# A two-by-two block scheme with seven products for the feed-forward of a hybrid trunk

## The chip, the cores and the metric

One Trainium2 chip, of which the kernel uses 1 core. The metric is the device time of one execution in microseconds, as the median of 3 runs.

## The reference

Two layers over 256 context tokens and 1024 latent tokens (1280 in all) of width 1024. Each layer is a mixer (layer 0: gated position mixing and grouped-query attention; layer 1: neighbourhood attention) and then a SwiGLU feed-forward with hidden width 2816. Both have a normed and modulated input and a normed and gated output:

```python
def swiglu(h, w_in, w_out):
    g, u = jnp.split(h @ w_in, 2, axis=-1)
    return (jax.nn.silu(g) * u) @ w_out
...
        fp = swiglu(sublayer_in(xp, norm_ffn_pre[l], fsh_p, fsc_p), ffn_w_in[l], ffn_w_out[l])
        fs = swiglu(sublayer_in(xs, norm_ffn_pre[l], fsh_s, fsc_s), ffn_w_in[l], ffn_w_out[l])
        xp = sublayer_out(xp, fp, norm_ffn_post[l], fgt_p)
        xs = sublayer_out(xs, fs, norm_ffn_post[l], fgt_s)
```

Everything is float32.

## The kernel before

**Precision.** A float32 product is made of three matrix products. `split` (L147 to L154) writes an operand as a high part (a cast, on ACT or DVE) and a low part (a subtraction of two SBUF tiles, on DVE or POOL), and `mm3_steps` (L168 to L170) adds high x high, high x low and low x high in PSUM.

**Feed-forward before.** The normed input lies transposed in the tiles `hh` and `hl` for the whole feed-forward (8 k tiles x 1280 tokens, both parts). A hidden tile `m` of 22 is 128 hidden columns: `wload` brings a gate unit, an up unit and an output unit (128 x 1024 each) from `wall` and splits them on ACT and POOL. `product` computes gate and up for a chunk of tokens (512, 512 or 256): 2 x 8 k tiles x 3 matmuls. `gating` takes silu, the product and a split. `output` multiplies each 128-token tile with the output unit, in two halves of 512 columns, 3 matmuls each, and DVE adds each half from PSUM to the running sum `y` (L1075), which stays in SBUF. So a hidden tile costs TensorE 48 weight tiles over 1280 tokens and 60 matmuls of 512 columns. The last three hidden tiles go chunk by chunk, so that the closing norms of the first chunks (L1090, L1097, L1105, and for layer 0 the transposes of `prenorm_cols`) go among the other chunks' products; in layer 0 the first products of the next mixer (`first_products`) go there too. `extra` makes six vectors of the modulation among the products of layer 0 and one in layer 1 (`mod_steps`, L224, on DVE).

**Ahead of it** `out_proj` goes tile by tile over 128 tokens; `cols` turns each normed tile into `hh` and `hl`, and for the last two tiles that step comes after the feed-forward's first item.

**Rooms.** The pools that matter: `s5` (17 tiles of 5 KB a partition), `wt` (8 of 4 KB), `raw` (3 of 4 KB), `t2` (5 of 2 KB), and eight PSUM banks: tag A (2 tiles of two banks), B (3 of one) and C (1). All transfers are issued from SP's queue. Outside the stretches whose order is written out by hand, a scheduler places the instructions of each engine by priority (program order) as their inputs come ready.

Of the kernel before, what the change touches and what calls it, by code (L numbers as in the profile page):

```python
# [18 lines left out]
P = 128  # L19
# [8 lines left out]
# So many of the feed-forward's hidden tiles come chunk by chunk.  # L28
LAST = 3
DEFER = 2  # L30
AFTER = 0
# [5 lines left out]
# Weight units of 128 x 1024 in the order of use.  # L37
# [12 lines left out]
def trunk_kernel(ctx: ExitStack, tc: tile.TileContext, A: dict, O: dict):  # L50
# [50 lines left out]
    # Scale and shift of the normed input: layer, sub-layer, condition, (A, B), k tile.  # L101
# [9 lines left out]
    # Sums over the partitions, to row 0 or row 1.  # L111
# [28 lines left out]
    def pipeline(items, *stages):  # L140
        """Each stage, (lag, function), on each item, lag steps behind the first."""
# [6 lines left out]
    def split(hi, lo, src, eng=None, hi_eng=None):  # L148
        """hi + lo = src, 12 bits each."""
# [14 lines left out]
    def mm3_steps(out, terms, per=1000):  # L164
        """Float32 products of operands that come as two 12-bit parts each."""
        n = len(terms)
        for i, (sh, sl, mh, ml) in enumerate(terms):
            PE.matmul(out, sh, mh, start=i == 0, stop=False)  # L168
            PE.matmul(out, sh, ml, start=False, stop=False)  # L169
            PE.matmul(out, sl, mh, start=False, stop=i == n - 1)  # L170
# [7 lines left out]
    def rstd_of(ss, n, scale, eps=EPS):  # L178
        """(ss * scale + eps) ** -0.5"""
        v, r = sm(n), sm(n)  # L180
        DVE.tensor_scalar(v, ss, scale, eps, op0=ALU.mult, op1=ALU.add)
        POOL.tensor_tensor(r, v, mhalf[:, 0:n], op=ALU.pow)  # L182
        return r

# [73 lines left out]

    def mods_of(*parts):
        return filler(itertools.chain(*(mod_steps(l, part) for l, part in parts)))  # L260

# [12 lines left out]
    def prenorm_cols(t, xh, l, w, wide, lo=None):  # L274
        """xh scaled, shifted and transposed, to hh and hl."""
# [15 lines left out]
    def gate_load(l, w, r):  # L291
        g = s5([P, D])
# [6 lines left out]
    def x_load(src):  # L299
        xt = raw([P, D])  # L300
        SP.dma_start(xt, src)
        return xt

    def postnorm(y, xt, gate, dst):
        """x + gate * normed y, to dst; returns it."""
# [3 lines left out]
        DVE.tensor_tensor(nx, nx, xt, op=ALU.add)  # L309
# [7 lines left out]
    def halves(base):  # L317
# [12 lines left out]
    def put_o(o, dst, base):  # L330
        """Sum of the two halves of o, to partitions base.. of dst."""
# [4 lines left out]
    class Job:  # L336
        """Heads' attention for two tiles of queries, step by step: keys on the free axis for the
        softmax, then turned in groups to meet the values."""

        def pair(self):  # L340
            """Room for two parts of a group."""
# [3 lines left out]
        def turn(self, i):  # L345
            """groups[i]: which output, and [(key tile, [(query tile, column)])]."""
# [43 lines left out]
    def run_jobs(jobs, slots, depth, extra, engines):  # L390
        """jobs(n): the n-th job or None at the end. Each goes on for depth periods of so many slots."""
# [21 lines left out]
    # ================= layer 0, mixer =================  # L413
# [34 lines left out]
    # Norm gains of keys and of queries, these times 1/8.  # L448
# [4 lines left out]
    def head_squares(n, src, nh, tmp):  # L453
        """Per-head norm, and rotary of latents, of src, [P, nh * 64] in PSUM: four parts."""
# [33 lines left out]
    def in_proj_rows(acc, t, units, nk, n):  # L488
        """acc[tok, n] = h W for one tile of tokens; units of nk k tiles each."""
# [7 lines left out]
    # Keys and values of both heads.  # L497
# [90 lines left out]
    def cache_steps():  # L588
        """The cache's keys and values."""
# [1094 lines left out]
```

## Time and profile before

| | |
|---|---|
| median of 3 runs | 3514.62 us (3513.19 to 3517.15) |
| profiled execution, span | 3511.9 us |
| TensorE (PE) busy | 3329.4 us, 95% |
| VectorE (DVE) busy | 2175.8 us, 62% |
| ScalarE (ACT) busy | 1319.9 us, 38% |
| GpSimd (POOL) busy | 1222.6 us, 35% |
| transfers | 260.19 MB, mean 74 GB/s |

The profiled execution's own time is known by its span, from the first to the last instruction; the runs' times hold the little that lies around it as well, so the median stands 2.7 us above the span. Feed-forward 0 runs from about 752 us to about 1724 us of the span, feed-forward 1 from about 2577 us to the end. A matmul's shown duration is a latency: matmuls overlap, and their cost is the distance from start to start.

### The profile page before, as it was taken

The numbers are of one execution on the slowest core, as the hardware profiler recorded it, in microseconds if no ns is written. First come the engines' busy times: TensorE is split into PE (matmuls) and PEld (weight loads), VectorE is DVE, ScalarE is ACT, GpSimd is POOL, SyncE is SP. The second block draws the span as 40 slices with busy tenths as digits, with TensorE's granted clock in tenths as the row PEclk, the third lists the DMA queues.
The fourth block names the chain that finished last, engine by engine and source line by source line (L and its number), as shares of the span: only waits on it lengthen the run. The fifth ranks groups of instructions, "written<-read, shape, count | busy, mean of one in ns | idle before, by whom it ended". The sixth has DMA issues, their size and how long they took to land. (4 is left out here: it accounts for less than half of the span.)

```text
span 3511.9 us, 46282 instructions
## 1 busy us (share of the span) xinstructions
PE 3329.4 (95%) x17930; PEld 2790.1 (79%) x17930; DVE 2175.8 (62%) x3749; ACT 1319.9 (38%) x2561; POOL 1222.6 (35%) x822
## 2 busy tenths in 40 slices
PE   6889899999999999999899999998999999999998
PEld 3667787887877878887788888887877888888886
DVE  7879998546666664445767777777574444443447
ACT  3467863441111111113666666666541111111123
POOL 3556666451111111124644444444221111111134
PEclk7889999999999999999999999999999999999999
DMA  5210033432222221113311111113331111111124
GB/s 207 65 37 13 19 95 123 155 123 85 90 86 81 85 86 39 44 51 132 124 40 45 44 45 44 45 44 102 108 131 57 36 37 36 39 45 38 37 85 167
DMA packets 106621, 260.19 MB, mean 74 GB/s; under 512 B 10640, under 2 KB 46352, under 8 KB 106400
## 3 DMA queue, kind: packets, MB, share of 16 engines
q1 hardware_dynamic: 106400, 257.23, 22.7%
q8 instruction: 141, 2.31, 0.3%
q14 instruction: 80, 0.66, 0.1%
HBM read 221.37 MB, written 35.82 MB: 73 GB/s over the span
## 5 line engine op out<-in xcount | busy, mean ns | idle before, releaser
L1075 DVE TENSOR_TENSOR s<-s,B 128x512 f32<-128x512 f32 x840 | 559.5, 684 | 568.2 <-PE B L170 567.3
L154 POOL TENSOR_TENSOR w<-raw,w 128x1024 fp32r<-128x1024 f32 x163 | 403.7, 2479 | 1412.0 <-ACT w L153 1406.9
L168 PE MATMUL A<-hh,w 128*128 128x512 f32 (+1 forms) x2112 | 755.5, 358 | 3.9 <-ACT w L153 2.4
L170 PE MATMUL A<-hh,w 128*128 128x512 f32 (+1 forms) x2112 | 750.4, 355 | 3.0 <-POOL w L154 3.0
L169 PE MATMUL A<-hl,w 128*128 128x512 f32 (+1 forms) x2112 | 747.9, 354 | 0.0
L168 PEld LDWEIGHTS A<-hh,w 128*128 128x128 f32 x2112 | 397.8, 188 | 69.8 <-issue 5.9
L170 PEld LDWEIGHTS A<-hh,w 128*128 128x128 f32 x2112 | 397.4, 188 | 66.4 <-POOL w L154 4.4
L169 PEld LDWEIGHTS A<-hl,w 128*128 128x128 f32 x2112 | 397.5, 188 | 62.8
L153 ACT CAST w<-raw 128x1024 fp32r<-128x1024 f32 x166 | 174.1, 1049 | 718.5 <-PE B L169 398.8
L168 PE MATMUL B<-w,s 128*128 128x512 f32 x880 | 351.2, 399 | 15.1 <-DVE s L1075 14.7
L170 PE MATMUL B<-w,s 128*128 128x512 f32 x880 | 348.1, 396 | 12.2 <-DVE s L154 10.2
L1056 ACT ACTIVATE t<-A,c 128x512 f32<-128x512 f32 (+1 forms) x132 | 81.1, 615 | 704.2 <-PE A L170 704.2
L169 PE MATMUL B<-w,s 128*128 128x512 f32 x880 | 344.1, 391 | 0.0
L352 PE MATMUL B<-c,s 128*128 128x128 f32 x1568 | 238.7, 278 | 40.4 <-DVE w L368 23.4
L368 DVE TENSOR_TENSOR t<-B,t 128x512 fp32r<-128x512 f32 (+1 forms) x248 | 162.3, 654 | 143.9 <-ACT t L362 140.3
L352 PEld LDWEIGHTS B<-c,s 128*128 128x128 f32 x1568 | 181.2, 141 | 83.2 <-DVE w L368 35.7
L168 PE MATMUL C<-hh,w 128*128 128x512 f32 (+1 forms) x576 | 211.6, 367 | 3.4 <-ACT s L1321 2.2
L1057 DVE TENSOR_TENSOR t<-t,A 128x512 f32<-128x512 f32 (+1 forms) x132 | 78.9, 597 | 217.4 <-ACT t L1056 217.4
L168 PEld LDWEIGHTS B<-w,s 128*128 128x128 f32 x880 | 165.4, 188 | 59.1 <-DVE s L1075 27.2
L170 PEld LDWEIGHTS B<-w,s 128*128 128x128 f32 x880 | 165.5, 188 | 55.3 <-DVE s L154 15.6
L170 PE MATMUL C<-hh,w 128*128 128x512 f32 (+1 forms) x576 | 205.3, 356 | 0.0
L169 PE MATMUL C<-hl,w 128*128 128x512 f32 (+1 forms) x576 | 205.0, 356 | 0.0
(285 smaller groups left out, 6473.1 us busy)
## 6 DMA issues: line engine op xcount, KB each, us to landing
raw<-wall SPq DMA_DIRECT2D x171, 512.0 KB, 3.5
raw<-mod_w SPq DMA_DIRECT2D x72, 512.0 KB, 4.0
x_d<-s SPq DMA_DIRECT2D x30, 512.0 KB
w<-wall SPq DMA_DIRECT2D x22, 512.0 KB, 3.7
raw<-x SPq DMA_DIRECT2D x20, 512.0 KB, 4.2
s<-x_d SPq DMA_DIRECT2D x20, 512.0 KB, 6.5
s<-wall SPq DMA_DIRECT2D x17, 512.0 KB, 6.0
w<-mod_w SPq DMA_DIRECT2D x16, 512.0 KB, 10.0
```

Source lines behind the costliest of these rows:

```text
L153: ACT.copy(hi, src)
L154: (eng or DVE).tensor_tensor(lo, src, f32(hi), op=ALU.subtract)
L168: PE.matmul(out, sh, mh, start=i == 0, stop=False)
L169: PE.matmul(out, sh, ml, start=False, stop=False)
L170: PE.matmul(out, sl, mh, start=False, stop=i == n - 1)
L352: PE.transpose(tr[:, at : at + P], self.p[a][:, col : col + P], ident)
L368: DVE.tensor_tensor(tl[:, 0:n], tr[:, 0:n], f32(th[:, 0:n]), op=ALU.subtract)
L1056: ACT.activation(s, acc[:, 0, 0:n], AF.Silu, bias=zerob)
L1057: DVE.tensor_tensor(s, s, acc[:, 1, 0:n], op=ALU.mult)
L1075: DVE.tensor_tensor(yt, yt, part, op=ALU.add)
```

## The change

For both matrix products of the feed-forward the operands are seen as two-by-two blocks, and the four block sums, of eight block products, are made from seven. The blocks of the tokens are even and odd tiles of 128 tokens, those of the inner axis are halves (k tiles 0 to 3 and 4 to 7; even and odd hidden tiles for the second product), those of the columns are gate and up (for the second product the two halves of 512).

- `prenorm_pair`: an odd tile's first four k tiles are stored as the difference to the even tile. `out_proj` goes in `OUT_ORDER`.
- Stage one (`step`, 22 hidden tiles): seven products of 4 k tiles x 3 matmuls, over token sets of 384 and of 256. Three operands more of the tokens (`sums`) lie in 12 of the 17 `s5` tiles. `weights` makes seven split operands of a hidden tile, `collect` the sums, the gating and the store of the inner activations to DRAM (`gu_d`), unsplit.
- Stage two: for two pairs of hidden tiles at a time `down_load` brings the activations and output units back, `down_split` makes the operands in `hh` and `hl`, which are free by then, and `group` goes over five pairs of token tiles in three groups of products. The eleventh pair of hidden tiles comes last, pair of token tiles by pair, with the closing norms behind each (`tail_...`). The next mixer's first products come in the program behind all that.
- `behind` holds the first instructions of the feed-forward behind the last ones of `out_proj` on their engines; `mod_half_steps` makes the modulation in halves of 512 columns.

```diff
+SETS = (slice(2, 5), slice(0, 2))
...
+    def prenorm_pair(t, xh, l, w, lo):
...
+        if t % 2 == 0:
+            split(hh[:, :, rows(t)], hl[:, :, rows(t)], xh, lo, DVE)
+        else:
+            split(hh[:, 4:8, rows(t)], hl[:, 4:8, rows(t)], xh[:, 4:8], lo, DVE)
+            for x in (hh, hl):
+                DVE.tensor_tensor(xh[:, 0:4], xh[:, 0:4], f32(x[:, 0:4, rows(t - 1)]), op=ALU.subtract)
+            split(hh[:, 0:4, rows(t)], hl[:, 0:4, rows(t)], xh[:, 0:4], lo, DVE)
...
+    PRODUCTS = ((1, 0), (5, 2), (2, 0), (3, 2), (6, 1), (7, 1), (4, 1))
+    def three(out, a, b, start):
...
+            for j, (x, z) in enumerate(((ah, bh), (ah, bl), (al, bh))):
+                PE.matmul(out, x, z, start=start and i + j == 0, stop=i == n - 1 and j == 2, skip_group_check=True)
...
+        more = [[[s5([P, 2, 640], F32R) for _ in range(2)] for _ in range(2)] for _ in range(3)]
+        def sums(s):
...
+            for k in range(4):
...
+                DVE.tensor_tensor(x, b22[0], t1[0], op=ALU.subtract)
+                DVE.tensor_tensor(d, b22[1], t1[1], op=ALU.subtract)
+                DVE.tensor_tensor(x, x, d, op=ALU.add)
+                split(*parts[0], x, DVE)
+                POOL.tensor_tensor(z, b21[0], x, op=ALU.subtract)
+                POOL.tensor_tensor(z, z, b21[1], op=ALU.add)
+                split(*parts[2], z, POOL)
+                for v in b11:
+                    DVE.tensor_tensor(x, x, v, op=ALU.subtract)
+                split(*parts[1], x, DVE)
...
+        def weights(m, i):
+            g, u = st["gu", m, 0], st["gu", m, 1]
+            if i == 5:
...
+            elif i == 3:
+                DVE.tensor_tensor(g[:, 1], g[:, 1], g[:, 0], op=ALU.subtract)
...
+            st["w", m, i] = o = wt([P, 2, 512], F32R)
+            split(o[:, 0], o[:, 1], src, POOL)
...
+            elif i == 6:
+                DVE.tensor_tensor(uv[:, 0], x, z[:, 0], op=ALU.add)
+                DVE.tensor_tensor(uv[:, 0], y, uv[:, 0], op=ALU.add)
+                ACT.activation(uv[:, 0], uv[:, 0], AF.Silu, bias=zerob)
+            elif i == 7:
+                DVE.tensor_tensor(uv[:, 1], x, z[:, 0], op=ALU.add)
+                POOL.tensor_tensor(z[:, 1], uv[:, 1], z[:, 1], op=ALU.add)
+                POOL.tensor_tensor(z[:, 1], uv[:, 0], z[:, 1], op=ALU.mult)
+            elif i == 4:
+                DVE.tensor_tensor(z[:, 0], x, z[:, 0], op=ALU.add)
+                DVE.tensor_tensor(z[:, 0], z[:, 0], z[:, 2], op=ALU.mult)
+                SP.dma_start(gu_d[l][m][:, :, c], z[:, 0:2])
...
+        def step(m, i, where):
+            for s in range(2):
+                product(m, i, where, s)
+                collect(m, i, s)
+            if m < MT - 1:
+                weights(m + 1, i)
+            extra(2 if i == 1 else 1)
+        for fn in before:
+            fn()
+        with behind(("SP", "DVE", "PE")):
+            weights_load(0)
+            for i, _ in PRODUCTS:
+                weights(0, i)
+            sums(0)
+            weights_load(1)
+            for i, where in PRODUCTS:
+                if i == 6:
+                    sums(1)
+                step(0, i, where)
...
+        PAIRS = (1, 2, 3, 4, 0)
+        GROUPS = (((1, 0), (2, 1)), ((5, 2), (3, 3)), ((6, 4), (7, 5), (4, 6)))
...
+        def down_ready(j, i):
...
+            if i == 5:
+                st["gs", j] = s5([P, 640])
+                DVE.tensor_tensor(st["gs", j], ge[:, 1], go[:, 1], op=ALU.add)
+                DVE.tensor_tensor(ge[:, 1], ge[:, 0], ge[:, 1], op=ALU.subtract)
+                DVE.tensor_tensor(ge[:, 0], st["gs", j], ge[:, 0], op=ALU.subtract)
+                POOL.tensor_tensor(we[:, 0], we[:, 1], we[:, 0], op=ALU.subtract)
+            elif i == 3:
+                DVE.tensor_tensor(go[:, 0], go[:, 0], ge[:, 0], op=ALU.subtract)
+            elif i == 6:
+                POOL.tensor_tensor(we[:, 1], wo[:, 1], we[:, 1], op=ALU.subtract)
+                POOL.tensor_tensor(wo[:, 1], wo[:, 1], we[:, 0], op=ALU.subtract)
+            elif i == 4:
+                POOL.tensor_tensor(wo[:, 0], wo[:, 0], wo[:, 1], op=ALU.subtract)
...
+        def down_split(js, g, at):
...
+                    split(ah[:, 0], ah[:, 1], a, POOL if g == 2 else DVE)
+                    split(bh[:, 0], bh[:, 1], b, POOL)
...
+        def group(g, ops):
...
+                three(banks[q], *cuts, k == 0)
+                down_collect(q, i, banks[q])
...
+        for c, js in enumerate(chunks):
+            for g in range(3):
+                now = ready
+                if g < 2:
+                    at = 8 - at
+                    ready = down_split(js, g + 1, at)
+                else:
...
+                group(g, now)
...
+        def tail_tokens(q):
...
+            for n, i in enumerate((1, 2, 5, 3, 6, 7, 4)):
+                a, _ = tail_ready(i, place[q])
+                o = ops[n // 4][:, n % 4]
+                split(o[:, 0], o[:, 1], a, DVE)
...
+        def tail_products(q):
...
+                three(banks[where], [(ops[i][:, 0], ops[i][:, 1])], [(tail_w[i][:, 0], tail_w[i][:, 1])], i in (1, 5, 6))
+                down_collect(q, i, banks[where])
+            z = first_sum[q]
+            POOL.tensor_tensor(e[:, 1], e[:, 1], z, op=ALU.add)
+            POOL.tensor_tensor(o[:, 1], o[:, 1], z, op=ALU.add)
+            DVE.tensor_tensor(o[:, 0], o[:, 0], z, op=ALU.add)
...
+        for n, q in enumerate(PAIRS):
+            if n + 1 < len(PAIRS):
+                tail_tokens(PAIRS[n + 1])
...
+            tail_products(q)
+            for t in (2 * q, 2 * q + 1):
+                tail_norm(t)
+                if l == 0:
+                    tail_cols(t)
```

`down_collect` adds a product's bank to its sum by one DVE instruction of 128x512, as L1075 does before. `weights` for product 5 has three sums of 128x512 on DVE. `tail_norm` has for each tile a square sum (ACT), one product with the gate (DVE or POOL, by turns) and one fused multiply and add (DVE).

## Rows read from the trace of the kernel before

**Rows 1.** The page: span, and busy time, share and instructions by engine.

```profile
span 3511.9 us, 46282 instructions
...
PE 3329.4 (95%) x17930; PEld 2790.1 (79%) x17930; DVE 2175.8 (62%) x3749; ACT 1319.9 (38%) x2561; POOL 1222.6 (35%) x822
```

**Rows 2.** The chain of work in layer 1: start us, us, what.

```profile
3030.07 0.24 PE B L168
...
3113.20 0.24 PE B L168
```

**Rows 3.** Busy us by engine in six hidden tiles of layer 1.

```profile
core 0: us, PE busy (x) PEld busy (x) DVE busy (x) ACT busy (x) POOL busy (x), PEclk, DMA share, GB/s
2904.90:3154.32 249.42, 249.42 (x1226) 209.22 (x1226) 101.07 (x157) 39.28 (x54) 43.37 (x18) 1.00 0.12 39
```

**Rows 4.** Timeline of PE: a run of 256 columns, then one of 512.

```profile
3070.76 0.28 PE L168 MATMUL A<-hh,w 128*128 128x256 f32 x1
...
3071.47 0.40 PE L168 MATMUL B<-w,s 128*128 128x512 f32 x1
...
3075.60 0.40 PE L168 MATMUL A<-hh,w 128*128 128x512 f32 x1
```

**Rows 5.** PE's waits, 750 to 1250 us: us in total, times, longest.

```profile
PE B L170 <- DVE s L154: 7.7, 4, 2.1
PE B L168 <- DVE s L1075: 2.6, 3, 1.5
```

**Rows 6.** Single lines: ns min/median/max of one, first and last start, forms.

```profile
L1075 DVE TENSOR_TENSOR s<-s,B x840: 666/686/690, 815.8 to 3502.2; 128x512 f32<-128x512 f32 x168
...
L154 POOL TENSOR_TENSOR w<-raw,w x163: 2333/2411/3553, 547.5 to 3489.9; 128x1024 fp32r<-128x1024 f32 x163
L154 DVE TENSOR_TENSOR s<-t,s x132: 411/692/2859, 765.6 to 3499.1; 128x512 fp32r<-128x512 f32 x88, 128x256 fp32r<-128x256 f32 x44
...
L486 DVE TENSOR_TENSOR t<-t x8: 277/2476/2489, 77.3 to 178.9; 128x128 f32<-128x128 f32 x8
...
L1090 DVE TENSOR_TENSOR s<-s,s x20: 1204/1215/3422, 1641.6 to 3504.0; 128x1024 f32<-128x1024 f32 x20
...
L1097 DVE SCALAR_TENSOR_TENSOR s<-s,sm,s x22: 742/1272/3382, 1648.3 to 3508.3; 128x1024 f32<-128x1024 f32 x18, 128x512 f32<-128x512 f32 x4
...
L271 DVE TENSOR_SCALAR s<-s,sm x20: 752/754/2881, 653.9 to 2583.2; 128x1024 f32<-128x1024 f32 x20
...
L641 DVE SCALAR_TENSOR_TENSOR t<-raw,c,t x28: 734/740/2827, 49.0 to 149.6; 128x512 f32<-128x512 f32 x28
```

**Rows 7.** Timelines of POOL and DVE where two operations meet.

```profile
2576.96 5.72 POOL L154 TENSOR_TENSOR w<-raw,w 128x1024 fp32r<-128x1024 f32 x2 [1.13 <-ACT w L153]
...
2577.19 3.23 DVE L309 TENSOR_TENSOR s<-s,raw 128x1024 f32<-128x1024 f32 x1
```

**Rows 8.** Timelines of ACT and DVE, start of feed-forward 0.

```profile
752.33 1.11 ACT L265 ACTIVATE t<-A,c 128x1024 bf16<-128x1024 f32 x1 [0.65 <-PE A L170]
...
756.10 1.23 DVE L309 TENSOR_TENSOR s<-s,raw 128x1024 f32<-128x1024 f32 x1
...
771.87 0.68 DVE L151 CAST hh<-s 128x1024 fp32r<-128x1024 f32 x1
```

**Rows 9.** Busy time by engine at three ends and starts.

```profile
1640.00:1680.00 40.00, 35.70 (x162) 28.14 (x160) 31.57 (x41) 24.56 (x54) 23.03 (x16) 0.96 0.45 158
1680.00:1720.00 40.00, 34.55 (x217) 30.15 (x217) 34.58 (x45) 21.87 (x33) 30.05 (x16) 1.00 0.59 206
1720.00:1760.00 40.00, 35.79 (x179) 27.92 (x178) 27.50 (x29) 28.67 (x70) 25.37 (x14) 1.00 0.19 66
2540.00:2580.00 40.00, 32.90 (x149) 25.62 (x148) 28.02 (x32) 23.64 (x51) 12.16 (x12) 0.96 0.43 145
...
3480.00:3512.00 32.00, 18.12 (x106) 14.28 (x104) 26.82 (x34) 9.14 (x15) 16.15 (x9) 0.90 0.50 186
```

**Rows 10.** The page: a DMA issue, count, KB, us to landing.

```profile
raw<-wall SPq DMA_DIRECT2D x171, 512.0 KB, 3.5
```

More of the change, by code (lines that the diff above doesn't have):

```diff
@@ L169, in mm3_steps @@
             PE.matmul(out, sh, ml, start=False, stop=False)
-            PE.matmul(out, sl, mh, start=False, stop=i == n - 1)
+            marks["PE"] = PE.matmul(out, sl, mh, start=False, stop=i == n - 1)
             if (i + 1) % per == 0 and i < n - 1:
@@ L183, in rstd_of, with behind @@
         return r
+    marks = {}
+    @contextmanager
+    def behind(names):
+        with ExitStack() as stack:
+            for n in names:
+                stack.enter_context(tc.issue_after(marks[n].ins))
+            yield
     def finish(gen):
@@ L257, in mod_steps, with mod_half_steps @@
         yield
+    def mod_half_steps(l, part, make):
+        w, what = part // 3, part % 3
+        for j in range(2):
+            total = [t2([P, 512]) for _ in range(2)]
+            for k in range(0, KT, 2):
+                r = make([P, 2, 512])
+                SP.dma_start(r, A["mod_w"][l, k * P : k * P + 256, part * D + 512 * j : part * D + 512 * j + 512].rearrange("(b p) n -> p b n", b=2))
+                yield
+                for b in range(2):
+                    for c in range(2):
+                        if k + b == 0:
+                            DVE.tensor_scalar(total[c], r[:, b], cond[:, k + b, c : c + 1], None, op0=ALU.mult)
+                        else:
+                            DVE.scalar_tensor_tensor(total[c], r[:, b], cond[:, k + b, c : c + 1], total[c], op0=ALU.mult, op1=ALU.add)
+                    yield
+            res, acc = t2([32, 512]), bank_c((32, 512))
+            SP.dma_start(res, A["mod_b"][l, part, 32 * j : 32 * j + 32])
+            for c in range(2):
+                PE.matmul(acc, pick[:, c, :], total[c], start=c == 0, stop=c == 1)
+            yield
+            DVE.tensor_tensor(res, acc, res, op=ALU.add)
+            if what == 2:
+                SP.dma_start(gate_d[l, w, :, 512 * j : 512 * j + 512], res[0:2])
+                yield
+                continue
+            tr = bank_c((P, 4, 32))
+            for b in range(4):
+                PE.transpose(tr[:, b, :], res[:, rows(b)], ident[0:32, 0:32])
+            yield
+            for r in range(2):
+                dst = mods[:, l, w, r, 1 - what, 4 * j : 4 * j + 4]
+                if what == 0:
+                    DVE.tensor_copy(dst, tr[:, :, r])
+                else:
+                    DVE.scalar_tensor_tensor(dst, tr[:, :, r], 1.0, gpre[:, l, w, 4 * j : 4 * j + 4], op0=ALU.add, op1=ALU.mult)
+            yield
     def mods_of(*parts):
-        return filler(itertools.chain(*(mod_steps(l, part) for l, part in parts)))
+        return filler(itertools.chain(*(mod_half_steps(l, part, s5) for l, part in parts)))
     def sumsq(src, n=D):
@@ L308, in postnorm @@
         DVE.scalar_tensor_tensor(nx, y, rs, gate, op0=ALU.mult, op1=ALU.mult)
-        DVE.tensor_tensor(nx, nx, xt, op=ALU.add)
+        marks["DVE"] = DVE.tensor_tensor(nx, nx, xt, op=ALU.add)
         SP.dma_start(dst, nx)
@@ L1023, in norms @@
         def norms(t):
-            nx = postnorm(st.pop(("y", t)), st.pop(("x", t)), gate[0 if t < 2 else 2], dst[rows(t), :])
+            nx = postnorm(st.pop(("y", t)), st.pop(("x", t)), gate[t < 2], dst[rows(t), :])
             st["xh", t] = prenorm_rows(nx)
         def cols(t):
-            prenorm_cols(t, st.pop(("xh", t)), l, 1, False, DVE if early else POOL)
-        pipeline(ORDER, (0, load), (1, product), (3 if early else 2, lambda t: t in ORDER[-DEFER:] or cols(t)), (1, norms))
-        return [lambda t=t: cols(t) for t in ORDER[-DEFER:]]
@@ new lines, in cols @@
+            prenorm_pair(t, st.pop(("xh", t)), l, 1, DVE if early else POOL)
+        late = OUT_ORDER[-2:]
+        pipeline(OUT_ORDER, (0, load), (1, product), (3 if early else 2, lambda t: t in late or cols(t)), (1, norms))
+        return [lambda t=t: cols(t) for t in late]
+    gu_d = [dr.tile([MT, P, 2, 640], F32, name=f"gu_d{l}") for l in range(2)]
+    hh5, hl5 = (x.rearrange("p k (q e f) -> p k q e f", e=2, f=P) for x in (hh, hl))
+    PRODUCTS = ((1, 0), (5, 2), (2, 0), (3, 2), (6, 1), (7, 1), (4, 1))
```

308 lines of the change are left out of this document (193 added, 115 removed).

## The prediction

> **What bounds the kernel now.** I read the page first: TensorE is busy for 3329.4 of 3511.9 us, no other engine for more than 62% [rows 1]. That is a mean over stages, so I went to the feed-forward. The chain of waits there is PE alone, and the same matmul comes back at 3030.07 and, two hidden tiles on, at 3113.20 [rows 2]: 41.57 us for a hidden tile. The windows say the same: over six of them, 249.42 us, PE has no idle time, DVE is busy for 41% and POOL for 17% [rows 3]. PE's timeline gives the price of a matmul from start to start. Six of 256 columns take 3071.47 - 3070.76 = 0.71 us, 0.119 us each; the 18 of 512 behind them take 4.13 us, 0.229 us each [rows 4]. A hidden tile is 48 weight tiles x (2 x 0.229 + 0.119) = 27.7 us and 60 x 0.229 = 13.7 us, in all 41.4 us, which is the period. So the feed-forward is bound by matmuls; twice 22 tiles are 1829 us of the span. What the reader has to carry along is the reverse: DVE and POOL have much room there now, and the change fills it.
>
> **What the change takes away.** Stage one has 7 x 4 x 3 = 84 weight tiles for each hidden tile, over 384 and 256 columns. No row has 384 columns; the bounds are 0.119 and 0.229 us [rows 4], and as 384 lies midway I take 0.174. Then a hidden tile costs 84 x (0.174 + 0.119) = 24.6 us instead of 27.7: 3.1 us, 68 us a layer. Stage two has 11 pairs x 7 products x 5 pairs of token tiles x 3 = 1155 matmuls of 512 columns instead of 1320: 165 x 0.229 = 38 us. Together 106 us a layer, 211 us in both. In layer 0 PE's waits for DVE of 7.7 and 2.6 us [rows 5] belong to code that goes: 10 us more. Sum of the gains: 221 us.
>
> **What it adds, and the port behind it.** TensorE's saving is paid with sums and splits on DVE, POOL and ACT. Prices [rows 6]: a POOL operation on two SBUF tiles takes 2.41 us for 1024 columns, so 1.5, 1.2, 0.9 and 0.6 us for 640, 512, 384 and 256. On DVE it takes 1.21 us for 1024, 0.69 for 512, 0.41 for 256, 0.28 for 128 (its least; most of those eight met POOL), so about 0.8 for 640 and 0.55 for 384. Adding a PSUM bank to a sum takes 0.69 us, with hardly any spread (666 to 690 ns). But DVE operations on SBUF alone reach 2.5 to 3.4 us, and the timelines show why: DVE's addition at 2577.19 takes 3.23 us instead of 1.2, as POOL's split began at 2576.96 [rows 7]. It ends about its own 1.2 us after the first POOL operation can have ended: the two don't overlap, one waits out the other. POOL's own maximum of 3553 ns is 2.41 plus one DVE operation of 1.2 us. So I add the times of such operations on both engines as if they were one resource. The Trainium skill says it as a rule, in "SBUF — State Buffer", "Who interferes with whom": the pair of ports that DVE and GpSimd share is an exclusive lock for a whole instruction, and a DVE instruction with two SBUF inputs takes part, one with at most one such input, outside two-port modes, doesn't. By that rule the sums below are floors, whatever the order; this trace agrees in both directions (3.23 us, and 0.69 us for L1075).
>
> **Start of a feed-forward.** In layer 0 the last mixer product ends by 752.33, when ACT reads it; DVE's last addition, the new mark, ends at 757.3, 5 us later, and the last transposed tile comes at 771.87 [rows 8]. Products 6, 7 and 4 of the first hidden tile need `sums(0)`: 28 DVE operations of 384 columns (15.4 us) and 12 on POOL (10.8 us), behind the 4 sums of weights (2.8 us), 6 more splits on POOL (7.2 us) and the last tile's steps (some 5 us on DVE, 2.4 on POOL). DVE alone: 5 + 23 = 28 us; with POOL's 20.4 us taken in full, 49 us. Until then PE has products 1, 5, 2 and 3: 12 matmuls each, 4 x (2.09 + 1.43) = 14.1 us, and two of the next hidden tile, 7 us. So PE idles for 28 - 21 = 7 to 49 - 14 = 35 us, and `sums(1)` (28 x 0.41 and 12 x 0.6 us) can add 6. I take 25 us in layer 0. In layer 1 PE is idle for 40 - 32.90 = 7 us there already [rows 9], so 18 more.
>
> **Stage one.** A hidden tile needs 7 x 1.2 + 2 x 0.9 + 2 x 0.6 = 11.4 us of POOL and about 4 us of DVE on that resource, in layer 0 another 6.5 us for the modulation (six vectors of 32 DVE operations of 0.74 us, over 22 tiles): at most 22 of 24.6 us. It fits, but product 7 adds to the bank that DVE must have read after product 6, and only the smaller set's product, 1.43 us, lies between. A late DVE stalls PE: nothing to 2 us a tile. I take 10 us in layer 0, 3 in layer 1 (0 to 40). The store (655 KB a tile) and the weights ride on a DMA share of 0.12 [rows 3]; behind the store in SP's queue stand weights that are needed a tile later.
>
> **The turn from stage one to two.** The loads of the first chunk (four tiles of 655 KB) wait for `s5` rooms that products 6, 7 and 4 hold to the end. 512 KB land in 3.5 us [rows 10]; 2.6 MB at the 206 GB/s of a dense stretch [rows 9] are 13 us, of which the last products cover some 7, and a first split follows. 8 us a layer (3 to 20).
>
> **Stage two.** For a chunk of two pairs PE needs 210 x 0.229 = 48.1 us. POOL: 22 operations of 512 and 6 of 640, 35.4 us. DVE: 16 operations of 640 on SBUF, 12.8 us, and 35 banks, 24.2 us. On the shared resource 48.2 us: as much as PE. The 9 split operands of the third group (23.4 us of POOL with their differences) must be ready within the second group's 13.7 us and the first products of their own. Five chunks: from 0 (perfect packing) to 12 us each (the resource used for 80%). Work is prepared a group ahead, so I stay near the lower end: 4 us, 20 us a layer.
>
> **The tail.** For a pair of token tiles PE needs 21 x 0.229 = 4.8 us, DVE 11 x 0.28 + 7 x 0.69 + 0.69 + 1.21 + 2 x 1.27 and small ones, 12.6 us. Layer 1: five pairs are 63 us, less 6 us made ahead, plus some 10 us of waiting for POOL (5 x 4.8 us of it): 67 us, and 3 for the last store. PE's 24 us leave 46 idle; before, the last 32 us had 14 [rows 9]. 32 us more (20 to 45). Layer 0 adds two tiles' turns: DVE's port operations come to 9.0 us a pair (0.75 us for L271 among them), POOL's to 9.6 us: 93 us, less 6. PE has 24 us, 10 of transposes and 16.5 of the next mixer's first products (72 x 0.229): 36 idle, against 14 in the three windows of before [rows 9]. 22 us more (5 to 45).
>
> **Sum.** Layer 0: 25 + 10 + 8 + 20 + 22 = 85. Layer 1: 18 + 3 + 8 + 20 + 32 = 81. 221 - 166 = 55 us: the profiled span goes from 3511.9 to 3457 us, the median, 2.7 us above it, to 3460 us. It is a small difference of two large numbers, and it says so in the range.
>
> **Rivals.** *The shared resource becomes the bound* (slower). The place is stage two: at 80% use a chunk takes 60 us rather than 52, ten chunks 80 us, and the start goes to its upper ends, 16 us a layer: 3460 + 80 + 32 = 3572 us. It decides from 62 us over my sum; by the chunks alone that is 58.3 us for one. For it: 48.2 us of such work in 48.1. The rule of "SBUF — State Buffer" in the Trainium skill points here. Against: POOL has no dependence on PSUM and can run ahead where rooms allow. *Everything packs* (faster): no stall in stages one and two, the start at its lower end; the tail and the turn remain, some 60 us: 3515 - 221 + 60 = 3354 us. For it: PE's queue before is without a gap where DVE is at 41%. *The products don't cost less*: if 384 columns run at the price of 512, 84 x 22 x 2 x 0.055 = 203 us are lost, 3663 us. Against it: 256 columns cost half of 512.
>
> **How the numbers follow.** The forecast as summed: 0.60, of which 0.07 ends within 0.2% (7 us, about what a measurement of this kernel can tell from no change) and the rest faster; its own range is 3400 to 3520. Everything packs: 0.15, faster. The resource as bound: 0.22, slower. Costly columns: 0.03, slower. So 0.68 faster, 0.07 same, 0.25 slower. The range leaves out the outer half of the packed case and of the bound case, and the costly columns: 3370 to 3560 us.
>
> **What would show it.** Right: hidden tiles of stage one at 24.6 us; matmuls of 384 columns 0.174 us apart; PE waiting for DVE's low parts some 25 us into each feed-forward; chunks of 50 to 54 us; in the last 70 us PE under half busy, DVE full. Wrong: a hidden tile over 26 us in layer 1 (the products, or the bank between 6 and 7), chunks near 48 or over 58 us, or a start that idles less than 7 or more than 40 us. A POOL and a DVE operation on SBUF that overlap at their short durations would take the ground from under the whole sum of additions.

## The result: 3742 us, 6.5% slower, and the profile after

The changed kernel takes 3742.36 us against 3514.24 us (medians; ratio 1.065, 95% interval 1.0633 to 1.0667). The forecast was 3460, its range ended at 3560: wrong in sign and size. One of the four runs of the changed kernel took 10850.79 us; the median of the other three is 3740.37 us.

The page of after, against [rows 1]:

```profile
span 3742.3 us, 50626 instructions
...
PE 3248.7 (87%) x18672; PEld 2838.4 (76%) x18672; DVE 2480.0 (66%) x4185; ACT 1571.2 (42%) x3213; POOL 1992.9 (53%) x1535
```

TensorE is busy for 81 us less, and the span is 230 us longer. POOL gained 770 us of busy time, DVE 304, and neither is full on the mean, so stages have to be looked at. The windows of after, where [rows 3 and 9] stood before (feed-forward 0: start, stage one, stage two, tail; then the same of feed-forward 1, with its turn from stage one to two as third row):

```profile
core 0: us, PE busy (x) PEld busy (x) DVE busy (x) ACT busy (x) POOL busy (x), PEclk, DMA share, GB/s
752.00:824.00 72.00, 35.54 (x161) 30.96 (x159) 66.46 (x79) 27.54 (x61) 50.18 (x39) 0.67 0.16 52
824.00:1417.00 593.00, 558.12 (x3623) 531.43 (x3623) 362.29 (x512) 171.46 (x330) 332.69 (x251) 0.98 0.33 109
...
1420.00:1730.00 310.00, 256.38 (x1045) 203.27 (x1045) 217.20 (x282) 81.71 (x140) 189.01 (x127) 0.91 0.21 73
1730.00:1890.00 160.00, 86.59 (x279) 60.95 (x278) 88.35 (x127) 65.88 (x153) 85.24 (x56) 0.65 0.25 88
2707.00:2786.00 79.00, 36.47 (x166) 31.80 (x164) 73.89 (x95) 31.89 (x71) 47.00 (x39) 0.66 0.20 61
2786.00:3323.00 537.00, 522.62 (x3488) 514.26 (x3489) 198.25 (x318) 162.25 (x313) 270.87 (x233) 0.99 0.24 74
3323.00:3340.00 17.00, 11.32 (x77) 11.04 (x76) 3.18 (x7) 8.18 (x16) 16.92 (x14) 0.90 0.41 154
3340.00:3662.00 322.00, 265.93 (x1045) 208.73 (x1046) 231.89 (x285) 83.46 (x143) 195.84 (x133) 0.90 0.22 74
3662.00:3742.00 80.00, 39.84 (x112) 23.39 (x110) 62.47 (x96) 19.18 (x44) 44.02 (x31) 0.69 0.40 138
```

Only layer 1's stage one comes near the forecast: PE busy for 97%, clock 0.99. In the starts and tails PE is busy for 46 to 54%, in stage two for under 83%, and the granted clock sinks with them. The saving itself is there. DVE's first addition of product 6 marks a hidden tile (layer 1):

```profile
3250.11 0.56 DVE L1199 TENSOR_TENSOR s<-A,s 128x384 f32<-128x384 f32 x1 [6.09 <-PE A L1115]
...
3275.53 0.56 DVE L1199 TENSOR_TENSOR s<-A,s 128x384 f32<-128x384 f32 x1 [6.09 <-PE A L1115]
```

25.42 us instead of the 41.57 us of [rows 2], which held the output product as well. The price of 384 columns, for which no row stood, is read from PE's timeline: 11 matmuls from 3005.05 to 3006.96, 0.174 us each.

```profile
3005.05 0.34 PE L1115 MATMUL B<-hh,w 128*128 128x384 f32 x1
...
3006.96 0.45 PE L1115 MATMUL B<-hh,w 128*128 128x384 f32 x2
3007.25 0.28 PE L1115 MATMUL B<-hl,w 128*128 128x256 f32 x1
```

**Where the time went.** I cut both traces where ACT first reads the last tile of `out_proj` (before 752.33 and 2572.96, after 752.68 and 2711.88). Layer 0 and the next mixer take 138.6 us more, the rest 91.5. With the forecast's gains (116 and 106 us) added, the additions are 255 and 197 us, where 85 and 81 were forecast. By stages, each against TensorE's ideal: first L1199 at 823.60 and 2786.39 (ideal 16.1 us after the cut; 7 us were idle before in layer 1), the last at 1396.38 and 3325.60 (ideal 517.4 us later); stage two's first matmul at 1420.16 and 3339.79 (ideal 7.9 us later); the tail's, 1050 matmuls on, at 1731.65 and 3663.30 (ideal 240.5 us later); the rest is the difference.

| us, layer 0 / 1 | forecast | measured |
|---|---|---|
| start | 25 / 18 | 55 / 51 |
| stage one | 10 / 3 | 55 / 22 |
| turn | 8 / 8 | 16 / 6 |
| stage two, beyond 48.1 a chunk | 20 / 20 | 71 / 83 |
| tail, with the next mixer's first products | 22 / 32 | 58 / 35 |
| sum | 85 / 81 | 255 / 197 |

The starts, stage one, stage two and layer 0's tail cost two to seven times what was forecast; the turn lies within its range, and layer 1's tail came out nearly as forecast. Of layer 0's 55 us in stage one some 12 were there before the change as well (the modulation's own work on TensorE, run 5), so its tail is dearer by as much.

**What stands in stage two.** PE's waits (layer 0, 1420 to 1730: us in total, times, longest), and what DVE itself waited for there:

```profile
PE B L1115 <- DVE s L1308: 46.5, 10, 14.4
```

```profile
DVE s L1263 <- POOL hl L153: 10.0, 2, 5.5
DVE s L1383 <- POOL hh L153: 8.6, 1, 8.6
DVE s L1263 <- POOL hh L153: 5.5, 1, 5.5
```

The timelines of POOL, DVE and PE show one such wait in layer 1:

```profile
3486.14 9.14 POOL L153 TENSOR_TENSOR hh<-s,hh 128x640 fp32r<-128x640 f32 x6
3495.18 1.32 POOL L153 TENSOR_TENSOR hh<-w,hh 128x512 fp32r<-128x512 f32 x1
3509.66 1.42 POOL L153 TENSOR_TENSOR hl<-raw,hl 128x512 fp32r<-128x512 f32 x1 [13.16 <-ACT hl L152]
...
3487.53 0.69 DVE L1308 TENSOR_TENSOR s<-A,s 128x512 f32<-128x512 f32 x1 [0.67 <-PE A L1115]
3493.83 3.36 DVE L1263 TENSOR_TENSOR s<-s,s 128x640 f32<-128x640 f32 x1 [5.61 <-POOL hh L153]
3497.11 0.68 DVE L1308 TENSOR_TENSOR s<-B,s 128x512 f32<-128x512 f32 x1
...
3501.48 0.81 DVE L1263 TENSOR_TENSOR s<-s,s 128x640 f32<-128x640 f32 x1
...
3488.68 1.52 PE L1115 MATMUL A<-hl 128*128 128x512 f32 x6
3497.94 5.46 PE L1115 MATMUL B<-hl 128*128 128x512 f32 x12 [7.73 <-DVE s L1308]
```

L1263 is the first sum of the next chunk. It stands in DVE's queue ahead of the second group's bank additions. It waits 5.61 us for POOL's low parts, and is then shown for 3.36 us beside POOL's last ones, where the next L1263 takes 0.81 us. The additions behind it had their products at hand, and PE had no bank left. POOL itself is idle for 13.16 us a moment later, so over a chunk there is room. This gave two theories: the work on the port is too much (A1, the rival on record), or one instruction stands in the wrong place in a queue (A2). A1 asks for less work, A2 only for another order.

### The profile page after: what moved, and what is told of

It is laid out like the page before. It is cut to its first block, busy times and chain, and to the rows that moved or that the text cites. A ratio compares the mean times of both kernels' runs of the same rounds, so it can differ in the third digit from the quotient of the medians.

```text
span 3742.3 us, 50626 instructions
## 1 busy us (share of the span) xinstructions
PE 3248.7 (87%) x18672; PEld 2838.4 (76%) x18672; DVE 2480.0 (66%) x4185; ACT 1571.2 (42%) x3213; POOL 1992.9 (53%) x1535
## 5 line engine op out<-in xcount | busy, mean ns | idle before, releaser
L153 POOL TENSOR_TENSOR w<-raw,w 128x512 fp32r<-128x512 f32 (+1 forms) x325 | 459.3, 1419 | 437.3 <-ACT w L152 437.3
L1115 PE MATMUL A<-s,w 128*128 128x384 f32 (+1 forms) x3168 | 502.6, 316 | 74.9 <-DVE s L1203 31.8
L1115 PEld LDWEIGHTS A<-s,w 128*128 128x128 f32 x3168 | 482.7, 192 | 93.9 <-DVE s L1203 38.8
L152 ACT CAST w<-raw 128x512 fp32r<-128x512 f32 (+1 forms) x328 | 203.9, 631 | 459.7 <-PE A L1115 373.1
L1115 PE MATMUL B<-hh,w 128*128 128x256 f32 (+1 forms) x1408 | 328.4, 315 | 22.5 <-ACT s L1193 20.1
L1115 PE MATMUL A<-hh,w 128*128 128x384 f32 (+1 forms) x1408 | 322.1, 310 | 16.1 <-ACT w L152 10.0
L1115 PEld LDWEIGHTS B<-hh,w 128*128 128x128 f32 x1408 | 248.6, 193 | 27.7 <-ACT s L1193 20.9
L1115 PEld LDWEIGHTS A<-hh,w 128*128 128x128 f32 x1408 | 241.7, 189 | 22.3 <-ACT w L152 11.5
L1115 PE MATMUL A<-hl,w 128*128 128x384 f32 (+1 forms) x704 | 217.5, 309 | 4.9 <-DVE hl L153 2.8
L1115 PE MATMUL B<-hl,w 128*128 128x384 f32 (+1 forms) x704 | 221.1, 314 | 0.0
L1199 DVE TENSOR_TENSOR s<-A,s 128x384 f32<-128x384 f32 x88 | 43.0, 489 | 191.7 <-PE A L1115 189.6
```

The lines of the kernel that those rows point to most:

```text
L152: ACT.copy(hi, src)
L153: (eng or DVE).tensor_tensor(lo, src, f32(hi), op=ALU.subtract)
L1115: PE.matmul(out, x, z, start=start and i + j == 0, stop=i == n - 1 and j == 2, skip_group_check=True)
```

## The experiments

Each kernel is the changed one with the edit shown, run beside the kernel before; 9 and 11 were timed in five rounds, the others once; three of the changed kernel's own runs lie within 5 us of each other. The experiments stand by subject, numbered by label, and "..." marks cuts in their code.

**1. POOL's low parts left out in stage two.** The matmuls read the high parts in their place, so results differ.

```diff
-split(ah[:, 0], ah[:, 1], a, POOL if g == 2 else DVE)
-split(bh[:, 0], bh[:, 1], b, POOL)
+if g == 2:
+    ACT.copy(ah[:, 0], a)
+else:
+    split(ah[:, 0], ah[:, 1], a, DVE)
+ACT.copy(bh[:, 0], b)
...
-    [(x[:, 0], x[:, 1]) for _, x in ops[i]],
+    [(x[:, 0], x[:, 0]) for _, x in ops[i]],
```

> Stage two without GpSimd's low parts (22 splits of 512 columns less their low part would be 35.4 us of POOL a chunk with the 8 differences; what is left are the 8 differences, 9.6 us); the matmuls read the high part in their place, so the number and size of the matmuls, the loads, the additions and DVE's work stay. A chunk of stage two takes 62 us (layer 0) and 64 us (layer 1) in the changed kernel, 48.1 us by its matmuls. If GpSimd's work on the shared port is what holds stage two (theory A), a chunk falls to 48 to 52 us: ten chunks, 110 to 150 us, so 3590 to 3630 us. If the passage through DRAM or the rooms hold it (theory B: loads that land late), a chunk stays over 58 us and the time over 3700 us. If VectorE's own bank additions and sums are too slow by themselves (theory C), the chunk falls by less than 5 us.

3621.11 us. A chunk (210 matmuls) takes 52.7 (layer 0) and 52.4 us (layer 1) on the mean, by PE's timeline; it was 62.3 and 64.7. Its stage two in layer 0:

```profile
1410.77:1674.41 263.64, 248.72 (x1053) 199.31 (x1051) 195.78 (x285) 82.98 (x142) 64.49 (x40) 0.98 0.26 90
```

The clock is back at 0.98, and the chunk falls by ten of its 62 us: theories B and C fall. But A1 and A2 both expect this.

**2. The next group's splits among this group's products**, one operand behind each bank addition instead of all ahead of the group (program order only).

```diff
-ready = down_split(js, g + 1, at)
+meanwhile = down_split(js, g + 1, at, ready)
...
+                next(meanwhile, None)
```

> Nothing is left out: the sums and splits of the next group of stage two stand in the program one operand at a time among this group's bank additions instead of all ahead of them. Theory A1, the sum of work on the port is too much (throughput): the work is the same, so a chunk stays at 60 to 64 us and the time within 15 us of 3742. Theory A2, the order: a bank addition stands on VectorE behind a sum that waits for GpSimd or for a room, though the port would have time for it: a chunk falls to 50 to 54 us, some 100 us in ten chunks, 3620 to 3660 us.

3726.26 us, chunks of 60.9 and 61.8 us on the mean. It reads like A1, but it did not test A2: the scheduler that orders each engine's instructions put L1263 ahead of the additions again, and DVE waits for POOL there as before (16.0 us in layer 0). Program order is not queue order in this kernel.

**6. The sums held in the queue.** With `issue_after`, the next chunk's L1263 to L1265 stand behind the last bank addition of the second group.

```diff
+with behind(("sum",) if "sum" in marks else ()):
     DVE.tensor_tensor(st["gs", j], ge[:, 1], go[:, 1], op=ALU.add)
     DVE.tensor_tensor(ge[:, 1], ge[:, 0], ge[:, 1], op=ALU.subtract)
     DVE.tensor_tensor(ge[:, 0], st["gs", j], ge[:, 0], op=ALU.subtract)
...
+if g == 1:
+    marks["sum"] = marks["add"]
```

> Nothing is left out. In stage two the next chunk's first sums (the three operations of product 5, L1263 to L1265) are held on VectorE behind the last bank addition of this chunk's second group; the work on every engine stays the same, and so does its sum on the port. In the changed kernel one of these sums stands ahead of the second group's additions, waits for GpSimd's low parts, and TensorE loses 5.5 to 9.2 us in eight of ten chunks and 14.5 in one, behind which the granted clock is at half. Theory A2 (the order: one instruction at the head of VectorE's queue): chunks fall from 62 to 52 to 54 us, 3640 to 3665 us. Theory A1 (the sum of the work on the port): the wait only moves, chunks stay over 59 us, over 3710 us.

3689.95 us: 52 us for an order. The middle three chunks (two to four) take 159.4 us instead of 186.6 in layer 0, 159.5 instead of 185.7 in layer 1. In layer 0, first after, then this kernel:

```profile
1480.21:1666.85 186.64, 155.11 (x631) 123.03 (x630) 131.69 (x157) 52.85 (x87) 125.58 (x84) 0.91 0.23 76
```

```profile
1479.66:1639.10 159.44, 147.62 (x631) 116.97 (x630) 124.44 (x157) 53.10 (x88) 129.21 (x84) 1.00 0.27 90
```

53.1 us a chunk with all of the work in place, POOL busy for 81% and the clock at 1.00. A1 falls for these chunks. The saving fell short of the expectation: the first chunk did not change (60 and 73 us), nor the fifth (65 us in both layers). In layer 0 the fifth keeps a wait of 14.5 us; there the tail's first sum stands ahead in the same way.

**3. No sums of the tokens** (products 6, 7 and 4 read other blocks of the same size; results differ).

```diff
-            if i in (6, 7, 4):
+            if i in (6, 7, 4) and False:
...
-            sums(0)
...
-                if i == 6:
-                    sums(1)
```

> The three operands of sums and differences of the tokens are not made, and products 6, 7 and 4 read other blocks of the same size; the 12 rooms that those operands hold are free as well, so the loads of stage two can start earlier. First product 6 of a feed-forward comes 55 us (layer 0) and 63 us (layer 1) after the last mixer product ends its place, plus the ideal 14 us. If the sums are the start's price (theory A), both starts shrink by 35 to 45 us each and the turn by up to 10 us each: 3640 to 3670 us. If the steps of the last tiles and the weights' seven splits set it (theory B), the starts shrink by under 15 us each: over 3700 us.

3676.11 us, in the gap between the two theories. The first hidden tile, from its first matmul to the end of its last, takes 41.1 and 36.7 us instead of 76.4 and 78.5 (ideal 24.6), so the starts give 35 and 42 us. The turn gave nothing: since all products now read `hh` and `hl` to the end, the first chunk had to wait for them (80 and 85 us), an effect of my edit.

**7. The sums on VectorE alone.**

```diff
-POOL.tensor_tensor(z, b21[0], x, op=ALU.subtract)
-POOL.tensor_tensor(z, z, b21[1], op=ALU.add)
-split(*parts[2], z, POOL)
+DVE.tensor_tensor(z, b21[0], x, op=ALU.subtract)
+DVE.tensor_tensor(z, z, b21[1], op=ALU.add)
+split(*parts[2], z, DVE)
```

> Nothing is left out: GpSimd's 12 operations of each set in the sums of the tokens go to VectorE, which has 40 instead of 28. If operations of the two engines on SBUF exclude each other (theory A, the prediction's), VectorE's operations of 384 columns fall from 1.2 to 1.6 us to 0.55 and the first set's sums from 28 x 0.55 + 12 x 0.9 = 26 us to 40 x 0.55 = 22: product 6 of the first hidden tile comes 4 to 20 us earlier in both layers, 3705 to 3735 us. If they run side by side and the long times have another cause (theory B), VectorE has 6.6 us more to do and the start gets longer by 5 to 10 us in each layer: 3750 to 3760 us.

3727.23 us; the first hidden tile takes 71.9 and 72.0 us, 4.6 and 6.5 less, although DVE has 40 operations instead of 28. Theory A holds, at the lower edge of what it gave. The timelines of after show why (DVE, then POOL):

```profile
779.00 1.61 DVE L1132 TENSOR_TENSOR s<-hh 128x384 f32<-128x384 f32 x1
780.54 1.35 DVE L1133 TENSOR_TENSOR s<-hl 128x384 f32<-128x384 f32 x1
781.81 0.55 DVE L1132 TENSOR_TENSOR s<-hh 128x384 f32<-128x384 f32 x1
782.28 0.55 DVE L1134 TENSOR_TENSOR s<-s 128x384 f32<-128x384 f32 x1
...
775.51 4.69 POOL L153 TENSOR_TENSOR w<-raw,w 128x512 fp32r<-128x512 f32 x3
780.16 1.31 POOL L153 TENSOR_TENSOR s<-s,s 128x384 fp32r<-128x384 f32 x1
782.91 1.27 POOL L1136 TENSOR_TENSOR s<-hh,s 128x384 f32<-128x384 f32 x1 [1.43 <-DVE s L1134]
```

While POOL works, an operation of 384 columns takes DVE 1.35 to 1.61 us; in POOL's pause from 781.5 to 782.9 it takes 0.55. These lines agree with the rule of the Trainium skill, "SBUF — State Buffer", "Who interferes with whom", that the ports shared by the two are locked for a whole instruction.

**5. A quarter of the modulation's multiplications** (results differ).

```diff
-for b in range(2):
+for b in range(2 if k == 0 else 0):
```

> Of the modulation that runs among stage one's products only the first 2 of the 8 k tiles of each half are multiplied on VectorE; 12 of 16 such operations are left out, so the vectors are not the reference's; the loads stay. A hidden tile of stage one takes 27.4 us in layer 0 (mean from the third on) and 24.7 us in layer 1 in the changed kernel. If the modulation on VectorE makes the difference (theory A), layer 0 falls to 25.0 us or less, 20 tiles by 2.4 us, 45 to 50 us: 3692 to 3700 us. If it is something else of layer 0, such as the modulation's loads that share the rooms and SP's queue with the weights (theory B), it stays over 26.8 us and the time over 3725 us.

3716.10 us, between the two. Layer 0's hidden tile (mean from the third on, by L1199) falls from 27.3 to 26.5 us; layer 1's takes 25.5 in after, not 24.7 as I had expected. PE's waits for L1200, 9.2 us in layer 0's stage one of after, are gone. So these multiplications are some 0.7 of the 1.8 us that layer 0 has over layer 1. The rest is TensorE's own work for the modulation, which this run leaves in: its sums over the partitions (groups of instructions from 752 to 1420 us, in the kernel before and in after: count, busy us, mean ns):

```profile
L232 PE MATMUL C<-s,c 128*32 128x512 f32 x48 | 11.5, 598 | 0.0
L287 PE MATMUL C<-t,c 128*32 128x512 f32 x48 | 22.8, 598 | 1.7 <-DVE t L282 1.7
```

With the transposes (3.4 us) these are 26 us, 1.2 a tile. For as many matmuls TensorE is busy twice as long as it was before the change, a price that the forecast did not have. The edit also leaves out steps, so the modulation ends sooner; behind it (from 1180 us on) layer 0's tiles take 25.5 us, as layer 1's do.

**4. The tail's transposes one pair later.**

```diff
 tail_products(q)
+if l == 0 and n:
+    for t in (2 * PAIRS[n - 1], 2 * PAIRS[n - 1] + 1):
+        tail_cols(t)
 for t in (2 * q, 2 * q + 1):
     tail_norm(t)
-    if l == 0:
-        tail_cols(t)
+if l == 0:
+    for t in (2 * PAIRS[-1], 2 * PAIRS[-1] + 1):
+        tail_cols(t)
```

> Nothing is left out: in the tail of layer 0 the norm and the transposes of a pair of token tiles stand behind the products of the next pair instead of ahead of them. If the tail is a chain in TensorE's order (products, norm, transposes that wait for it, and only then the next pair's last products; theory A), the period of a pair falls from 26.6 us to under 18 and the time by 35 to 50 us: 3692 to 3707 us. If DVE's and GpSimd's work on the port sets it (theory B; 18.6 us a pair by the prediction's prices, so 93 us against the 114 us that the tail's products take), the time falls by less than 20 us.

3721.52 us, between the two. In after PE's own queue was the chain: the next pair's products stand behind transposes that wait for a norm.

```profile
1812.94 1.97 PE L332 MATMUL B<-c,s 128*128 128x128 f32 x8 [6.58 <-DVE s L1429]
1814.56 1.63 PE L1115 MATMUL B<-w,s 128*128 128x512 f32 x3
...
1831.08 1.94 PE L332 MATMUL B<-c,s 128*128 128x128 f32 x8 [12.46 <-DVE sm L180]
```

With the edit the tail's products span 73 us instead of 113. But half of the 40 us is given back: PE now waits for the last pair's norm at the end.

```profile
1803.45 0.96 PE L1115 MATMUL B<-w,s 128*128 128x512 f32 x3 [0.24 <-DVE t L1308]
1819.38 3.87 PE L332 MATMUL B<-c,s 128*128 128x128 f32 x16 [14.96 <-DVE sm L180]
```

**10. All four repairs at once** (6, 7, 4, and the tail's first sums held in the same way).

> Nothing is left out. The changed kernel, blocks in both stages, with the orders repaired: the next chunk's sums and the tail's held behind the second group's additions, the sums of the tokens on VectorE alone, the transposes of the tail one pair later. If these are separate losses, their single gains add up (52 + 15 + 21) and the tail's hold gives 5 to 15 us more: 3640 to 3650 us, still some 130 us over the kernel before, since the rest of the start, the turn and the tail stays. If they overlap, 3660 to 3690 us.

3639.53 us: they add up. Chunks two to five of layer 0 take 208.1 us, 52.0 each, and the wait before the tail is gone. In layer 1 they take 220.7 us: in the fifth PE still waits 11.6 us, as the bank additions stand behind a split (L153) that waits 9.0 us for ACT's copy. It is still 127 us over the kernel before.

**8. Blocks in stage one only.** The stored activations are split for two hidden tiles and multiplied in the ordinary way, 6 matmuls to a bank; the last four hidden tiles go token tile by token tile with the norms behind each.

```diff
+for ms, nxt in zip(parts, parts[1:]):
+    for m in nxt:
+        down_load(m)
+        down_split(m)
+    for t in ORDER:
+        down_product(ms, t)
```

> The changed stage one with an ordinary stage two: the stored activations come back, are split for two hidden tiles at a time and multiplied with the output units without blocks (1320 matmuls of 512 columns a layer instead of 1155), 6 to a bank; the last four hidden tiles go token tile by token tile, 12 matmuls to a bank, with the closing norms behind each. TensorE has 38 us more to do in each layer; VectorE has 17 us for 27.5 us of TensorE and GpSimd 4.8. Theory A (stage two and the tail lose their time to the block scheme's sums and splits on VectorE and GpSimd): stage two runs at TensorE's 302 us a layer with under 15 us of waits, the tail shrinks to some 20 us; 125 us less in layer 0 and 85 us in layer 1, 3520 to 3545 us. Theory B (the passage through DRAM and the turn between the stages lose it): stage two has over 40 us of waits a layer, over 3600 us.

3549.36 us, 4 us above theory A's range: 193 us less than the changed kernel, with 330 matmuls of 512 columns more. Stage two's windows, layers 0 and 1:

```profile
1410.00:1660.00 250.00, 246.68 (x1080) 203.10 (x1079) 166.31 (x225) 42.46 (x56) 48.39 (x20) 0.99 0.28 97
3228.00:3480.00 252.00, 248.01 (x1082) 203.78 (x1083) 169.16 (x228) 45.58 (x60) 50.31 (x21) 0.99 0.29 102
```

The passage through DRAM costs next to nothing there: PE is busy for 98% and more. So what is still over the kernel before had to be looked for in the starts and in stage one.

**9. The same, with DVE's load spread**: sums on DVE, half of the modulation in stage two, two output units split into `s5` rooms.

```diff
-extra(2 if i == 1 else 1)
+extra(i in (1, 2, 6, 4))
...
 down_product(ms, t)
+extra(2 if t == 2 else 1)
```

> Nothing is left out. The kernel with the ordinary stage two (3549 us) with three more edits: the sums of the tokens on VectorE alone, half of the modulation's steps moved from stage one to stage two (where VectorE has 17 us of work for 27.5 us of TensorE), and the last two output units split into rooms that leave the next mixer's weights their own. Theory A (what is left over before is VectorE's work in stage one and the start): 6 us for each start, 1.0 to 1.4 us for each of 20 tiles in layer 0, some 10 us for the weights that the next mixer's first products waited for, 40 to 50 us: 3500 to 3510 us, level with the kernel before or just under it. Theory B (moved work comes back as waits in stage two): 3535 to 3550 us.

3519.90 us against 3512.03 (ratio 1.0024, 1.0015 to 1.0034): nearly level, 10 us short of the expectation. The first hidden tile still takes 66.7 and 67.5 us.

**11. The sums of the tokens on TensorE.**

```diff
+for j, (x, z) in enumerate([(eye[0], v) for v in plus] + [(eye[1], v) for v in minus]):
+    PE.matmul(out, x, z, start=j == 0, stop=j == 3, skip_group_check=True)
+split(*part[i], out.rearrange("p (q f) -> p q f", f=P), DVE)
```

> Nothing is left out. The kernel of the run before (ordinary stage two, 3520 us), but the sums and differences of the tokens are made by TensorE, which idles there: four matmuls each with the unit matrix or its negative as the stationary operand, summed in PSUM (96 matmuls for each feed-forward, 14 us at 0.174 and 0.119 us); ACT and VectorE only split the sum out of PSUM, 24 operations on VectorE instead of 80, and none with two SBUF inputs. In the kernel of the run before the first hidden tile takes some 70 us in place of 24.6, VectorE is busy for 73 of the 81 us there. Theory A (VectorE's sums on the locked port are the start's price): the first hidden tile takes 24.6 + 14 us and some 5 us of waits, 20 to 28 us less in each layer: 3465 to 3485 us, under the kernel before by about 1%. Theory B (the start is bound by the chain of last norm, transposes, weights and rooms that stands ahead of the sums): under 8 us less in each layer, 3505 to 3520 us.

3483.65 us against 3512.84: ratio 0.992 (0.9907 to 0.9934), 0.8% faster than the kernel before. The first hidden tile takes 42.9 and 41.0 us; in its window DVE is busy for 33.20 of 49 us, where it was 66.74 of 72 in run 9 (752 to 824 us):

```profile
752.00:801.00 49.00, 37.15 (x228) 36.06 (x227) 33.20 (x50) 27.08 (x62) 22.03 (x16) 0.86 0.21 76
```

The start was held by DVE's sums of the tokens, as theory A says, but not by the port alone: in run 9, from 785.6 to 803.4 us, DVE makes them one behind the other in 0.55 and 0.42 us each, their own time, while POOL waits (DVE, then POOL):

```profile
790.34 0.55 DVE L1134 TENSOR_TENSOR s<-s 128x384 f32<-128x384 f32 x1
803.39 5.52 POOL L153 TENSOR_TENSOR w<-raw,w 128x512 fp32r<-128x512 f32 x2 [18.74 <-DVE s L153]
```

The gain is 36 us against run 9, less than the first tile suggests: its first matmul now comes 14 us after the last mixer product, where it was 6.6 and 7.7. The clock in the window rose as well, from 0.72 to 0.86, and its part is not told apart.

## Why the prediction was wrong

- **What bounds the kernel, and the gains**: right. 384 columns cost 0.174 us; layer 1's hidden tile took 25.42 us for 24.6; with the order repaired, chunks took 52 to 53 us, as the forecast had them. The rival of costly columns is out.
- **The port**: right as a mechanism (run 7). As a bound of stage two it is wrong: the rival's 60 us a chunk were nearly the measured 62.3 and 64.7, but with all of the work in place and another order 53.1 us were enough, close to my own 52. The rival hit the number for stage two for a reason that run 6 refutes.
- **Stage two, the step that failed**: "Work is prepared a group ahead, so I stay near the lower end." I priced operations as if they could go as soon as the port is free, and never asked what stands behind an instruction that waits on an in-order queue. One sum (L1263) ahead of bank additions cost 5.5 to 9.1 us in six of the ten chunks, and the tail's first sum 14.4 us in a seventh, plus the slow clock behind them; I had 4 us a chunk and measured 14 and 17. The order alone gave 52 us back (run 6).
- **Start**: mechanism right, size wrong. I took 25 us out of 7 to 35; it is 55, outside my bounds. I let PE fill the wait with products 1, 5, 2, 3 and two of the next hidden tile, but product 2 itself waited 8.6 and 11.5 us for ACT's copy of product 1, as ACT's queue held casts of sums that DVE had not made yet. Leaving the sums out gave 35 and 42 us.
- **Stage one**: I expected the bank between products 6 and 7 to cost at most 2 us a tile and took 10 and 3 us in all. It is 27.3 us a tile in layer 0 and 25.5 in layer 1 instead of 24.6. In layer 1 PE waits some 0.5 us a tile for L1203, the bank between products 7 and 4, which I had not named. In layer 0 the modulation's multiplications add some 0.7 us a tile and its own work on TensorE 1.2 (run 5), of which half was there before the change.
- **Turn**: 16 and 6 us for 8, within its range. Layer 0's holds one wait of 11.5 us of the same kind: L1203 of the last hidden tile stands on DVE behind a split of stage two that itself waits 9.42 us for ACT's copy.

```profile
1411.85 5.19 DVE L153 TENSOR_TENSOR hh<-s,hh 128x640 fp32r<-128x640 f32 x1 [9.42 <-ACT hh L152]
1416.96 0.41 DVE L1203 TENSOR_TENSOR s<-A,s 128x256 f32<-128x256 f32 x1
```

- **Tail**: sized as throughput of DVE and POOL (87 us in layer 0). The queue order on PE made it a chain; run 4 took 40 us off the products, of which 21 reached the end. Layer 1's 35 us are near the 32 of the forecast.
- **The clock**: not in the sum at all. The mean granted clock went from 0.984 to 0.933; twice the missing share of the span is the time at 1.2 GHz, some 112 us before and 501 us after. It follows the waits: stage two has 0.91 and 0.90 with them, 0.98 without POOL's low parts, 1.00 in run 6's middle chunks. I did not run a kernel that holds the clock through a wait, so its share in the 228 us is not told apart from the waits that bring it. A bound can be estimated: by the traces' clock records PE was busy for 84 us at 1.2 GHz before and for 273 us after; at 2.4 GHz that work would have taken about half (a matmul of 512 columns 0.23 instead of 0.43 us, see the end), so at most some 95 us of the 228 are the clock's.
- **The form of the sum**: 221 less 166 was called a small difference of large numbers, but the range let each addition vary within bounds that only knew throughput. Nearly all missed on the same side, so the misses added instead of cancelling. Queue order is shown as the cause in stage two (6) and in layer 0's tail (4), DVE's sums in the starts (3, 11); the four repairs together give back 103 of the 286 us by which the additions exceeded the forecast, and the rest is not shared out.

Left open: the first chunk of layer 1 (73 us, also after the repairs), and what holds the starts beyond the sums of the tokens.

## What to carry to other kernels

A saving on the engine that is the bound has to be weighed against in-order queues, not only against the busy shares of the engines that pay for it: for each added instruction that can wait, name what stands behind it on its engine, and hold it there by an explicit order, since program order alone need not set it. Take the half of a change whose side work fits (here stage one), leave the half whose saving (38 us a layer) is smaller than its bookkeeping, and let an engine that idles anyway do the sums: TensorE with a unit matrix was cheaper than 80 operations on VectorE. Terms that are all priced near their floor miss together instead of cancelling, and the range has to say so.

## What the hardware showed that I had not expected

An operation that waits for the port is shown as busy: 1.61 us where 0.55 are its own (run 7), 3.36 where 0.81 are (stage two). So the sum of two busy shares says little about whether there is room: in run 6's middle chunks POOL's 129.21 and DVE's 124.44 us make 254 us in a window of 159, and PE is busy for 93%. Some 72 us of DVE's are the 105 bank additions, which take their 0.69 us beside POOL as well. By the forecast's prices without waiting, an estimate, port work comes to 48.2 us a chunk, so there the port was in use for some 90% of the time without holding PE up, where the rival had taken 80% as the limit.

A wait costs more than its length. In the window from 1820 to 1850 us of after, in which PE is busy for 7.69 of 30 us, the granted clock is 0.50. PE's timeline behind the last wait there: matmuls of 512 columns are 0.43 us apart (1.2 GHz), and 0.23 us (2.4 GHz) only later.

```profile
1852.71 0.80 PE L169 MATMUL C<-hh,w 128*128 128x512 f32 x1 [6.58 <-POOL w L153]
...
1857.57 0.63 PE L168 MATMUL C<-hl,w 128*128 128x512 f32 x1
1858.00 0.63 PE L169 MATMUL C<-hh,w 128*128 128x512 f32 x1
...
1859.30 0.40 PE L167 MATMUL C<-hh,w 128*128 128x512 f32 x1
1859.53 0.39 PE L168 MATMUL C<-hl,w 128*128 128x512 f32 x1
```
